# Modulation vectors as TensorE products, a reordered seven-product scheme, and an earlier start of the second FFN half

## The chip, the cores and the metric

One core of one Trainium2 chip. The metric is the device time of one execution, in microseconds (us). TensorE (PE) multiplies matrices, VectorE (DVE) and GpSimd (POOL) work elementwise, ScalarE (ACT) applies functions and copies, SyncE (SP) issues the DMAs, in the order of its one queue.

## The reference, cut to what matters

Two blocks run one after the other on a sequence of 512 tokens of width 1024. The first has two layers of FFN, attention mix, FFN on the sequence and on a context of 256 tokens; the second has a recurrent and a stick-breaking layer and is not touched. What the change touches:

```python
c_act, cc_act = silu(c), silu(c_ctx)                     # two vectors of 1024
mod   = (c_act  @ w_mod[layer] + b_mod[layer])           # 9 vectors of 1024 a layer
mod_c = (cc_act @ w_mod[layer] + b_mod[layer])           # the same for the context
y = swiglu(modulate(rms_norm(h, g_pre), shift, scale), w1, w2)   # silu(gate) * up, then @ w2
h = h + 0.5 * gate * rms_norm(y, g_post)                 # hidden width 2816 = 22 blocks of 128
```

## The kernel before, in words

Everything is fp32. A large product is three fp32r products of a high and a low part (`mm3`, L415): each weight tile is cast by ScalarE into its high part (L348) and the rest is formed by VectorE or GpSimd (L354) in a ring of 8 tiles `op`. Weights come through a ring of 4 tiles `raw`. TensorE runs its instructions in the order in which the program emits them; a small planner with a clock of its own (`run`) interleaves generators for it. The other engines and the SP queue get their order from the framework's scheduler.

Four FFN sublayers take part, called F1 to F4 here: (layer 0, sub 0), (0, 2), (1, 0), (1, 2). Each walks its 22 hidden blocks in groups of 4, 4, 4, 3, 3, 4 (`ffn`, L694). The first group is computed plainly (`ffn1`, `ffn2`), beside the norms that are still pending. For the other five groups, `strassen` (L734) forms every hidden block from seven half-size products of twelve matmuls each, 84 in all: 384 columns wide in F1 to F3, 256 in F4. `wsums` (L386) forms the sums of weights they need. VectorE joins the products (L738, L749) while four PSUM banks b1 to b4 are reused: b1, b3 and b4 take a second product once VectorE or ScalarE has read the first. Then `ffn2` multiplies the group's blocks with the second weight matrix (the "second half" of the group below), eight output tiles m, for the context (256 columns) and the sequence (512); output tile m = 0 is begun with all blocks but the last.

The modulation vectors for later sublayers are made in the background. `tick` (L427), called between blocks and between output tiles, starts a piece of `mods` (L597): two loads of 512 KB of `w_mod` come through the `raw` ring, and VectorE multiplies it by one element of `c` per partition and adds it into `macc` (L624, L626), some instructions at a time (`drip`, L434). TensorE then sums `macc` over the partitions by a product with ones (L634), and four transposes (L647) bring the vector into feature order. The first two vectors of layer 0 are made otherwise (`mods0`, L569): products of 32 columns of `c` with 512 columns of `w_mod`, four side by side in the array (`tile_position`), L578.

Of the kernel before, what the change touches and what calls it, by code (L numbers as in the profile page):

```python
# [11 lines left out]
F32 = mybir.dt.float32  # L12
# [100 lines left out]
def layout(inp):  # L113
# [7 lines left out]
    o["wmodA"] = np.ascontiguousarray(wm[0, ..., : 2 * D])  # L121
    o["wmodB"] = np.ascontiguousarray(wm.reshape(2, 2, 4, P, 18, 512).transpose(0, 4, 1, 3, 2, 5))
# [142 lines left out]
class Builder:  # L265
    def __init__(self, ctx, tc, I, O):
        self.ctx, self.tc, self.nc, self.I, self.O = ctx, tc, tc.nc, I, O
        self.const = self.pool(ctx, "const")
        self.wp = self.pool(ctx, "wp")
        self.tmp = self.pool(ctx, "tmp")  # L270
        self.ps = ctx.enter_context(tc.tile_pool(name="ps", bufs=1, space=PSUM))
        self.wide = None
        self.open_wide()
        self.bg, self.drips = [], []
# [111 lines left out]
    def wsums(self, src):  # L386
# [16 lines left out]
        add(s1, a21, a22)  # L403
        add(s2, s1, a11)
        o2 = put(s2, False)
        add(a21, a11, a21)
        o3 = put(a21, True)
        o4 = put(a12, False)
        add(s2, s2, a12)
        o5 = put(s1, True)  # L410
        o6 = put(a22, True)
        o7 = put(s2, True)
# [21 lines left out]
    def drip(self, n):  # L434
        for f in self.drips[:n]:
            f()
        del self.drips[:n]
# [131 lines left out]
    def mods0(self, pool, hook):  # L569
# [4 lines left out]
        def step(k):  # L574
            raw = pool.tile([P, 2048], F32, name="raw", tag="raw", bufs=7)
            self.dma(raw, I["wmodA"][k])
# [20 lines left out]
    def mods(self, vectors):  # L597


        nc, I = self.nc, self.I  # L600
        box = {}

        def step(l, q, u, half):
            nv = 1 if l == 1 and q > 4 else 2
            if u == half == 0:
                box["po"] = self.po()
            raws = []

            def load():
                raws.append(self.raw())  # L610
                self.dma(raws[-1].rearrange("p (k c) -> p k c", k=2), I["wmodB"][l, 2 * q + u, half][:, 2 * len(raws) - 2 : 2 * len(raws)])

            load()
            if half == 0:
                box["acc"] = self.sums.tile([P, 2, 512], F32, name="macc", tag="macc", bufs=1)
            acc = box["acc"]

            def part(kk, v):
                k = 4 * half + kk
                if kk == 1 and v == 0:  # L620
                    load()
                w, c = raws[kk // 2][:, 512 * (kk % 2) : 512 * (kk % 2) + 512], self.cT[:, k, v : v + 1]
                if k == 0:
                    nc.vector.tensor_scalar(out=acc[:, v, :], in0=w, scalar1=c, scalar2=None, op0=ALU.mult)  # L624
                else:
                    nc.vector.scalar_tensor_tensor(out=acc[:, v, :], in0=w, scalar=c, in1=acc[:, v, :], op0=ALU.mult, op1=ALU.add)  # L626

            return [lambda kk=kk, v=v: part(kk, v) for kk in range(4) for v in range(nv)]

        def reduce(l, q, u):  # L630
            nv = 1 if l == 1 and q > 4 else 2
            po = box["po"][:, 256 * u : 256 * u + 256]
            for j in range(2 * nv):
                nc.tensor.matmul(po[32 * j : 32 * j + 32, :], lhsT=self.ones[:, 0:32], rhs=box["acc"][:, j % nv, j // nv * 256 : j // nv * 256 + 256],  # L634
                                 start=True, stop=True, tile_position=(0, 32 * j))
            if u:
                m = 64 * nv
                box["row"] = self.ftile(512, "row")
                nc.vector.tensor_copy(box["row"][:m, :], box["po"][:m, :])

        def finish(l, q):
            nv = 1 if l == 1 and q > 4 else 2
            m = 64 * nv
            row = box["row"]
            tp = self.pt()
            for b in range(4):
                nc.tensor.transpose(tp[:, b * P : b * P + m], row[:m, b * P : (b + 1) * P], self.ident[:m, :m])  # L647
            src = tp.rearrange("p (u b j w) -> p u b j w", u=2, b=2, w=32)
            two = lambda t: t.rearrange("p (h b) -> p b h", h=2)
            for v in range(nv):  # L650
                for u in range(2):
                    sl = slice(8 * q + 4 * u, 8 * q + 4 * u + 4)
                    nc.vector.tensor_tensor(out=two(self.modc[l][:, v, sl]), in0=src[:, u, :, v : 2 * nv : nv, 0],
                                            in1=two(self.small1[:, 72 * l + 8 * q + 4 * u :][:, :4]), op=ALU.add)
            if q % 3 == 1:
                self.mod_finish(l, q // 3)
            if q % 3 == 2:
                self.mod_gate(l, q // 3)

        def do(red, fin, now):  # L660
            if red:
                reduce(*red)
            if fin is not None:
                finish(*fin)
            return step(*now) if now else []

        out, last = [], None
        for x in vectors:
            for u in range(2):
                out.append(lambda a=last, b=(*x, u, 0): do(a, None, b))  # L670
                out.append(lambda a=last[:2] if last and not u else None, b=(*x, u, 1): do(None, a, b))
                last = (*x, u)
        out.append(lambda: do(last, None, None))
        out.append(lambda: do(None, last[:2], None))
        return out
# [18 lines left out]
    def ffn(self, l, sub, firsts, parts, joint, lasts, pend, exits, spill=None, lag=0):  # L694
# [6 lines left out]
        with self.tc.tile_pool(name=f"ffn{l}{sub}", bufs=1, reuse_waits="tile") as pool:  # L701
            self.fpool = self.sums = pool
            self.open_wide(True)
            i0 = off = 0
# [29 lines left out]
    def strassen(self, pool, l, wi, i0, mids, h):  # L734
# [4 lines left out]
        new = lambda nm: pool.tile([P, n], F32, name=nm, tag=nm, bufs=2)  # L739
        for ii, mid in enumerate(mids):  # L740
            A = self.wsums(self.I["wf1"][l, wi, i0 + ii])
            b1, b2, b3, b4 = (self.bank()[:, :n] for _ in range(4))

            def mm(i, p, b, start):
                yield from self.mm3(p, A[i], [(k, *x) for k, x in enumerate(b)], start=start, more=not start)
                self.drip(1)
# [8 lines left out]
            yield from mm(1, b2, h.T2, True)  # L755
            v = new("v")
            sub(v, b2, c)
            yield from mm(2, b3, h.T3, True)
            u = new("u")
            sub(u, v, b3)  # L760
            yield from mm(3, b1, h.B21, False)
            sg = pool.tile([P, 512], F32, name="sg", tag="sg", bufs=2)[:, :n]
            nc.scalar.activation(sg, b1, AF.Silu)
            yield from mm(4, b4, h.T1, True)
            sub(u, u, b4)
            yield from mm(5, b3, h.T4, False)
            m = self.ftile(n, "m")
            sub(m, v, b3)
            emit(0, m, sg)
            yield from mm(6, b4, h.B22, False)  # L770
# [4 lines left out]
            if ii % 2 == 0:  # L775
                yield from self.tick()

    def ffn1(self, pool, l, wi, i0, mids, ss, ticks=False):
        nc = self.nc
        for ii, mid in enumerate(mids):  # L780
# [3 lines left out]
            for w in (wg, wu):  # L784
                for st in ss:
                    p = self.pg()[:, : st.n]
                    yield from self.mm3(p, w, st.rhs())
                    if w is wg:
                        sg = pool.tile([P, 512], F32, name="sg", tag="sg", bufs=2)[:, : st.n]
# [6 lines left out]
                    if ticks:  # L796
                        self.drip(2)
# [3 lines left out]
    def ffn2(self, l, wi, off, mids, ss, first, last, ticks, cb=None):  # L801
        nc = self.nc
        n = 2 * len(mids) * P
        for m2 in range(4):
# [3 lines left out]
            for mm in range(2):  # L808
                m = 2 * m2 + mm
                rhs = lambda st: [(i, t[:, 0, st.cs], t[:, 1, st.cs]) for i, t in enumerate(mids)]  # L810
                ps = [self.pg()[:, : st.n] for st in ss] if m == 0 else []
                for st, p in zip(ss, ps):
                    yield from self.mm3(p, ws[mm], rhs(st)[:-1], stop=False)
                for i, st in enumerate(ss):
                    if m == 0:
                        p = ps[i]
# [11 lines left out]
                    if ticks:  # L828
                        self.drip(4 // len(ss))
# [408 lines left out]
    def block1(self):  # L1238
# [67 lines left out]
        pend = self.ffn(0, 0, first, [lat], both, both, pend, links(0, 0, 0, 1), lambda out: spill(out, True))  # L1306
        assert not self.bg
        pend = self.mix(0, both, both, pend, [link(cx, 0, 1, 0, 2), halves(0, 1, 0, 2)])
        self.bg += self.mods([(0, 8)] + [(1, q) for q in range(4)])
        pend = self.ffn(0, 2, first, [lat], both, both, pend, [link(cx, 0, 2, 1, 0), halves(0, 2, 1, 0)], spill)  # L1310
        assert not self.bg
        self.bg += self.mods([(1, q) for q in range(4, 8)])
        pend = self.ffn(1, 0, first, [lat], both, both, pend, links(1, 0, 1, 1), spill)
        assert not self.bg
        self.bg += self.mods([(1, 8)])
# [631 lines left out]
```

## Time and profile before

| | |
|---|---|
| time, median of 3 runs (lowest to highest) | 3959.23 us (3951.5 to 3959.98) |
| profiled execution: its time, its span | 3959.93 us, 3958.2 us |
| busy in the span: PE, DVE, ACT, POOL | 89%, 71%, 43%, 38% |
| mean granted clock of TensorE | 0.949 |
| VectorE busy on `macc` (L624, L626) | 382 us in 448 instructions |

The profiled execution has 1.7 us outside its span. The time of a stretch is compared with what its matmuls take when nothing is waited for; the rest is waiting, a lower clock, or small other work.

### The profile page before, as it was taken

What the parts mean: (1) busy time and instruction counts of PE and PEld (TensorE: products, weight loads), DVE (VectorE), ACT (ScalarE), POOL (GpSimd) and SP (SyncE); (2) the same over time, 40 slices, a digit from 0 to 9 for tenths busy, and PEclk for the clock granted to TensorE, in tenths of its full rate; (3) what the DMA queues carried; (4) which work ended last, traced back from release to release, by engine and by line L of the source; (5) the groups of instructions that cost most, each with busy time, mean ns of one, the idle gap of its engine ahead of it and who ended that gap; (6) DMA issues with size and microseconds to landing.
All of it is one profiled execution on the core that took longest, in us unless ns stands there. A gap on an engine that the chain in (4) does not pass through costs nothing. (4 is left out here: it accounts for less than half of the span.)

```text
span 3958.2 us, 61299 instructions
## 1 busy us (share of the span) xinstructions
PE 3529.9 (89%) x23004; PEld 3168.0 (80%) x23004; DVE 2821.9 (71%) x5221; ACT 1693.7 (43%) x3591; POOL 1491.1 (38%) x1191
## 2 busy tenths in 40 slices
PE   7798888999979898988999988988999888899997
PEld 6688788777778887877888976777888787899886
DVE  6977787766787878688767577667756777556446
ACT  5422224556543322344222344554334545535544
POOL 4534344321244433435434432124545434334112
PEclk8999999999989999989999989999999989999998
DMA  7333333312242323433333241133323320234112
GB/s 254 117 101 110 109 112 130 108 61 85 94 134 91 123 92 116 136 128 111 107 107 120 72 146 59 62 101 112 115 88 109 113 80 28 86 103 144 59 49 75
DMA packets 125440, 410.39 MB, mean 104 GB/s; under 512 B 14035, under 2 KB 25814, under 8 KB 123350
## 3 DMA queue, kind: packets, MB, share of 16 engines
q1 hardware_dynamic: 125142, 406.47, 31.8%
q8 instruction: 180, 2.95, 0.3%
q14 instruction: 118, 0.97, 0.1%
HBM read 397.90 MB, written 8.52 MB: 103 GB/s over the span
## 5 line engine op out<-in xcount | busy, mean ns | idle before, releaser
L354 POOL TENSOR_TENSOR op<-raw,op 128x512 fp32r<-128x512 f32 (+1 forms) x660 | 928.0, 1407 | 1595.3 <-ACT op L348 1459.9
L348 ACT CAST op<-raw 128x512 fp32r<-128x512 f32 (+2 forms) x1178 | 702.9, 606 | 796.3 <-DMA raw<-wf 351.8
L354 DVE TENSOR_TENSOR op<-raw,op 128x512 fp32r<-128x512 f32 (+2 forms) x518 | 447.7, 866 | 198.0 <-ACT op L348 194.9
L422 PE MATMUL pg<-h,op 128*128 128x256 f32 (+1 forms) x1440 | 477.4, 332 | 56.8 <-ACT sg L790 20.5
L422 PE MATMUL pg<-mid,op 128*128 128x256 f32 (+1 forms) x1264 | 453.7, 359 | 45.5 <-ACT mid L348 37.6
L424 PE MATMUL pg<-h,op 128*128 128x256 f32 (+1 forms) x1440 | 460.6, 320 | 12.5 <-DVE op L354 10.3
L423 PE MATMUL pg<-h,op 128*128 128x256 f32 (+1 forms) x1440 | 466.5, 324 | 5.7 <-DVE h L534 4.4
L423 PE MATMUL pg<-mid,op 128*128 128x256 f32 (+1 forms) x1264 | 447.1, 354 | 15.4 <-POOL mid L354 10.8
L424 PE MATMUL pg<-mid,op 128*128 128x256 f32 (+1 forms) x1264 | 443.2, 351 | 0.6 <-POOL op L354 0.6
L417 PE MATMUL bank<-h,op 128*128 128x384 f32 (+1 forms) x1704 | 319.2, 338 | 59.3 <-DVE u L738 53.7
L422 PEld LDWEIGHTS pg<-h,op 128*128 128x128 f32 x1440 | 291.3, 202 | 78.4 <-ACT sg L790 21.7
L626 DVE SCALAR_TENSOR_TENSOR macc<-raw,cT,macc 128x512 f32<-128x512 f32 x392 | 344.5, 908 | 12.4 <-DMA raw<-wmodB 11.7
L417 PEld LDWEIGHTS bank<-h,op 128*128 128x128 f32 x1704 | 293.4, 197 | 69.1 <-DVE u L738 31.0
L422 PEld LDWEIGHTS pg<-mid,op 128*128 128x128 f32 x1264 | 247.6, 196 | 99.0 <-ACT mid L348 45.3
L424 PEld LDWEIGHTS pg<-h,op 128*128 128x128 f32 x1440 | 291.2, 202 | 28.0 <-DVE op L354 11.3
L423 PEld LDWEIGHTS pg<-h,op 128*128 128x128 f32 x1440 | 290.9, 202 | 25.3 <-DVE h L534 13.1
L423 PEld LDWEIGHTS pg<-mid,op 128*128 128x128 f32 x1264 | 248.0, 196 | 49.8 <-POOL mid L354 15.6
L424 PEld LDWEIGHTS pg<-mid,op 128*128 128x128 f32 x1264 | 247.9, 196 | 31.8 <-POOL op L354 1.1
L825 DVE TENSOR_TENSOR y<-pg,y 128x256 f32<-128x256 f32 (+1 forms) x288 | 161.0, 560 | 144.1 <-PE pg L424 141.7
L354 POOL TENSOR_TENSOR op<-ws,op 128x512 fp32r<-128x512 f32 x142 | 212.8, 1499 | 129.3 <-ACT op L348 128.4
L348 ACT CAST op<-ws 128x512 fp32r<-128x512 f32 x213 | 131.8, 619 | 279.0 <-DVE ws L394 178.5
L422 PE MATMUL bank<-h,op 128*128 128x384 f32 (+1 forms) x636 | 208.1, 327 | 0.0
(427 smaller groups left out, 8545.5 us busy)
## 6 DMA issues: line engine op xcount, KB each, us to landing
raw<-wf SPq DMA_DIRECT2D x326, 512.0 KB, 3.8
raw<-wmodB SPq DMA_DIRECT2D x128, 512.0 KB, 3.8
raw<-win SPq DMA_DIRECT2D x58, 512.0 KB, 3.7
raw<-ewin SPq DMA_DIRECT2D x48, 512.0 KB, 3.7
raw<-owin SPq DMA_DIRECT2D x40, 512.0 KB, 3.7
raw<-wout SPq DMA_DIRECT2D x32, 512.0 KB, 3.6
raw<-wf SPq DMA_DIRECT2D x32, 384.0 KB, 3.2
raw<-ewout SPq DMA_DIRECT2D x24, 512.0 KB, 3.6
```

Of the source, the lines that this page charges most:

```text
L348: self.nc.scalar.copy(hi, src)
L354: eng.tensor_tensor(out=lo, in0=src, in1=hi.bitcast(F32), op=ALU.subtract)
L417: mm = self.nc.tensor.matmul if not more else lambda *a, **kw: self.nc.tensor.matmul(*a, skip_group_check=True, **kw)
L422: mm(p, lhsT=a, rhs=xh, start=start and i == 0, stop=False)
L423: mm(p, lhsT=a, rhs=xl, start=False, stop=False)
L424: mm(p, lhsT=b, rhs=xh, start=False, stop=stop and i == len(rhs) - 1)
L626: nc.vector.scalar_tensor_tensor(out=acc[:, v, :], in0=w, scalar=c, in1=acc[:, v, :], op0=ALU.mult, op1=ALU.add)
L825: nc.vector.tensor_tensor(out=y, in0=p, in1=y, op=ALU.add)
```

## The change

Three edits, all in the FFN sublayers:

- `mods` makes two vectors at a time as products on TensorE, the way `mods0` does. A step is 1 MB of `w_mod` (128 rows of two vectors) in two tiles `mraw` of their own and four products of 32 x 512 columns into `po`; eight steps make a pair, then ScalarE copies `po` to `row`, and at the next tick four transposes follow. The tiles for step i + 1 are loaded behind the matmuls of step i, into the same two tiles. The first load of an FFN is emitted at its start. `tick` runs one step; `strassen` calls it after every block (before: every second one), `ffn2` as before after its first three tile pairs. `drip` goes. The vector (1, 8), made in F4 before, is made in F3.
- `strassen` runs its seven products in another order: B11, T1, T2, T3, B21, B22, T4 (before B11, T2, T3, B21, T1, T4, B22), with `wsums` in the matching order. The half of the block that needs no second Silu comes last, and the last block of a group gets its low part from VectorE instead of GpSimd.
- `ffn2` begins output tile m = 1, too, with all blocks but the last, in PSUM banks of the `bank` ring.

```diff
 def wsums(self, src):
         add(s1, a21, a22)
+        o2 = put(s1, True)
         add(s2, s1, a11)
-        o2 = put(s2, False)
+        o3 = put(s2, False)
...
 def tick(self):
-        self.drip(99)
         if self.bg:
-            self.drips = self.bg.pop(0)()
-            yield 0.5
+            self.bg.pop(0)()
+            yield 0.9
...
+    def mods(self, pairs):
+        todo = [(pr, k) for pr in pairs for k in range(KD)]
+        def load(i):
+            pr, k = todo[i]
+            box[i] = [self.sums.tile([P, 1024], F32, name="mraw", tag="mraw", bufs=2) for _ in range(2)]
+            for t, (l, q) in zip(box[i], pr):
+                self.dma(t, I["wmod"][l, k][:, D * q : D * (q + 1)])
+        def step(i):
+            k = todo[i][1]
+            if k == 0:
+                box["po"] = self.po()
+            if i not in box:
+                load(i)
+            raws = box.pop(i)
+            for j in range(4):
+                nc.tensor.matmul(box["po"][32 * j : 32 * j + 32, :], lhsT=self.cT[:, k, :], rhs=raws[j // 2][:, 512 * (j % 2) : 512 * (j % 2) + 512],
+                                 start=k == 0, stop=k == KD - 1, tile_position=(0, 32 * j))
+            if k == KD - 1:
+                box["row"] = self.stile(512)
+                nc.scalar.copy(box["row"], box["po"])
+            if i + 1 < len(todo):
+                load(i + 1)
...
 def strassen(self, pool, l, wi, i0, mids, h):
-        new = lambda nm: pool.tile([P, n], F32, name=nm, tag=nm, bufs=2)
+        new = lambda nm: pool.tile([P, n], F32, name=nm, tag=nm, bufs=1)
...
-                self.split(mid[:, 0, c0 : c0 + n], mid[:, 1, c0 : c0 + n], a, True)
+                self.split(mid[:, 0, c0 : c0 + n], mid[:, 1, c0 : c0 + n], a, ii < len(mids) - 1)
...
+            yield from mm(1, b4, h.T1, True)
+            yield from mm(2, b2, h.T2, True)
             v = new("v")
             sub(v, b2, c)
             u = new("u")
-            sub(u, v, b3)
+            sub(u, v, b4)
+            yield from mm(3, b3, h.T3, True)
+            sub(u, u, b3)
+            yield from mm(4, b1, h.B21, False)
...
+            yield from mm(5, b4, h.B22, False)
             m = self.ftile(n, "m")
             sub(m, b4, v)
             nc.scalar.activation(m, m, AF.Silu)
             emit(n, u, m)
-            if ii % 2 == 0:
-                yield from self.tick()
+            yield from mm(6, b3, h.T4, False)
+            m = self.ftile(n, "m")
+            sub(m, v, b3)
+            emit(0, m, sg)
+            yield from self.tick()
...
 def ffn2(self, l, wi, off, mids, ss, first, last, ticks, cb=None):
-                ps = [self.pg()[:, : st.n] for st in ss] if m == 0 else []
-                for st, p in zip(ss, ps):
-                    yield from self.mm3(p, ws[mm], rhs(st)[:-1], stop=False)
+                if m == 0:
+                    ps = {(x, i): (self.bank if x else self.pg)()[:, : st.n] for x in range(2) for i, st in enumerate(ss)}
+                    for (x, i), p in ps.items():
+                        yield from self.mm3(p, ws[x], rhs(ss[i])[:-1], stop=False)
...
 def block1(self):
-        self.bg += self.mods([(0, q) for q in range(2, 8)])
+        self.bg, loads = self.mods([((0, q), (0, q + 1)) for q in (2, 4, 6)])
...
+        self.bg, loads = self.mods([((0, 8), (1, 0)), ((1, 1), (1, 2)), ((1, 3), (1, 4))])
...
+        self.bg, loads = self.mods([((1, 5), (1, 6)), ((1, 7), (1, 8))])
```

## Rows read from the trace of the kernel before

**Rows 1.** The page's busy times: busy us, share of the span, instructions.

```profile
PE 3529.9 (89%) x23004; PEld 3168.0 (80%) x23004; DVE 2821.9 (71%) x5221; ACT 1693.7 (43%) x3591; POOL 1491.1 (38%) x1191
```

**Rows 2.** Windows, the 15 seven-product stretches of F1 to F3: length, busy (instructions).

```profile
290.80:361.90 71.10, 61.73 (x350) 59.34 (x349) 62.24 (x78) 25.82 (x50) 38.21 (x27) 1.00 0.37 117
...
2229.20:2288.40 59.20, 59.20 (x337) 59.16 (x337) 34.35 (x45) 24.81 (x46) 30.93 (x25) 1.00 0.32 102
sum 912.60, PE 846.07 PEld 823.44 DVE 668.63 ACT 341.00 POOL 495.37; mean PE 56.40 PEld 54.90 DVE 44.58 ACT 22.73 POOL 33.02
```

**Rows 3.** The same windows, instructions on tile macc alone: length, PE, PEld, DVE.

```profile
290.80:361.90 71.10, 0.64 (x8) 0.16 (x8) 21.90 (x23) 1.00 0.37 117
...
2229.20:2288.40 59.20, 0.00 (x0) 0.00 (x0) 0.00 (x0) 1.00 0.32 102
sum 912.60, PE 8.00 PEld 1.94 DVE 160.68; mean PE 0.53 PEld 0.13 DVE 10.71
```

**Rows 4.** Windows, the 12 second halves between those stretches; columns as in rows 2.

```profile
sum 425.80, PE 392.31 PEld 321.40 DVE 314.42 ACT 52.09 POOL 74.19; mean PE 32.69 PEld 26.78 DVE 26.20 ACT 4.34 POOL 6.18
```

**Rows 5.** Waits of PE from 183 to 2342 us: us in total, times, longest.

```profile
PE bank L417 <- DVE u L738: 51.2, 23, 5.1
...
PE pg L422 <- ACT mid L348: 22.0, 12, 3.7
...
PE pg L423 <- POOL mid L354: 9.8, 15, 0.7
```

**Rows 6.** Waits of PE from 2757 to 3100 us, in F4.

```profile
PE bank L417 <- DVE u L738: 13.3, 11, 2.4
PE pg L422 <- ACT mid L348: 11.0, 4, 3.8
```

**Rows 7.** Timeline of PE behind a wait, then across a sum of two vectors' macc.

```profile
2811.73 0.63 PE L422 MATMUL pg<-mid,op 128*128 128x512 f32 x1
2812.16 0.63 PE L423 MATMUL pg<-mid,op 128*128 128x512 f32 x1
...
2815.09 0.40 PE L423 MATMUL pg<-mid,op 128*128 128x512 f32 x1
2815.33 0.40 PE L424 MATMUL pg<-mid,op 128*128 128x512 f32 x1
2815.65 0.62 PE L634 MATMUL po<-macc,ones 128*32 128x256 f32 x4
2816.21 0.50 PE L422 MATMUL pg<-mid,op 128*128 128x512 f32 x1
```

**Rows 8.** Timeline of PE: the same sum with four column groups, in F1.

```profile
263.19 0.64 PE L634 MATMUL po<-macc,ones 128*32 128x256 f32 x8
263.76 0.39 PE L422 MATMUL pg<-mid,op 128*128 128x256 f32 x1
```

**Rows 9.** Timeline of PE at the start: steps of mods0 (a step is x8).

```profile
19.37 4.01 PE L578 MATMUL po<-raw,cT 128*32 128x512 f32 x24
...
30.02 1.94 PE L578 MATMUL po<-raw,cT 128*32 128x512 f32 x8 [4.24 <-DMA raw<-wmodA]
```

**Rows 10.** Windows, F4: sums over its 5 seven-product stretches, then its 4 second halves.

```profile
sum 190.10, PE 176.76 PEld 173.75 DVE 130.24 ACT 92.28 POOL 124.78; mean PE 35.35 PEld 34.75 DVE 26.05 ACT 18.46 POOL 24.96
...
sum 101.40, PE 89.41 PEld 68.05 DVE 55.95 ACT 25.45 POOL 36.59; mean PE 22.35 PEld 17.01 DVE 13.99 ACT 6.36 POOL 9.15
```

**Rows 11.** Window, the first group of F1, all instructions; columns as in rows 2.

```profile
81.90:183.80 101.90, 77.47 (x497) 69.14 (x497) 96.30 (x142) 43.82 (x91) 52.80 (x36) 0.93 0.40 132
```

**Rows 12.** DMA issues: count, KB each, median us from issue to landing.

```profile
raw<-wf SPq DMA_DIRECT2D x326, 512.0 KB, 3.8
...
ac<-xc SPq DMA_DIRECT2D x2, 1024.0 KB, 3.9
xc<-ac SPq DMA_DIRECT2D x2, 1024.0 KB, 6.2
```

**Rows 13.** Waits of the SP queue over the span: us in total, times, longest.

```profile
SPq L286 <- DVE op L354: 2452.9, 467, 29.3
```

More of the change, by code (lines that the diff above doesn't have):

```diff
@@ L575, in step @@
             raw = pool.tile([P, 2048], F32, name="raw", tag="raw", bufs=7)
-            self.dma(raw, I["wmodA"][k])
+            self.dma(raw, I["wmod"][0, k][:, : 2 * D])
             for j in range(4):
@@ L595, in mods0 @@
         return out
-    def mods(self, vectors):
+    def mods(self, pairs):
         nc, I = self.nc, self.I
         box = {}
-        def step(l, q, u, half):
-            nv = 1 if l == 1 and q > 4 else 2
-            if u == half == 0:
-                box["po"] = self.po()
[L607 to L644, printed above, removed]
@@ L645, in finish @@
+        def finish(pr):
             tp = self.pt()
             for b in range(4):
[L647 to L672, printed above, removed]
@@ L673, in mods @@
-        out.append(lambda: do(last, None, None))
-        out.append(lambda: do(None, last[:2], None))
-        return out
+                nc.tensor.transpose(tp[:, b * P : (b + 1) * P], box["row"][:, b * P : (b + 1) * P], self.ident)
+            src = tp.rearrange("p (b j w) -> p j b w", b=4, w=32)
+            for i, (l, q) in enumerate(pr):
+                for v in range(1 if l == 1 and q > 4 else 2):
+                    nc.vector.tensor_tensor(out=self.modc[l][:, v, 8 * q : 8 * q + 8].rearrange("p (j b) -> p j b", b=4), in0=src[:, 2 * i : 2 * i + 2, :, v],
+                                            in1=self.small1[:, 72 * l + 8 * q :][:, :8].rearrange("p (j b) -> p j b", b=4), op=ALU.add)
+                if q % 3 == 1:
+                    self.mod_finish(l, q // 3)
+                if q % 3 == 2:
+                    self.mod_gate(l, q // 3)
@@ L677, in mod_finish @@
+        out = []
+        for i, (pr, k) in enumerate(todo):
+            out.append(lambda i=i: step(i))
+            if k == KD - 1:
+                out.append(lambda pr=pr: finish(pr))
+        load_first = lambda: load(0)
+        return out, load_first
     def mod_finish(self, l, sub):
@@ L691, in mod_gate, with ffn @@
                                            scalar=1.0 if sub == 1 else 0.5, in1=gq, op0=ALU.mult, op1=ALU.mult)
-    def ffn(self, l, sub, firsts, parts, joint, lasts, pend, exits, spill=None, lag=0):
+    def ffn(self, l, sub, firsts, parts, joint, lasts, pend, exits, spill=None, lag=0, first=None):
         wi = 0 if sub == 0 else 1
@@ L703, in ffn @@
             self.open_wide(True)
+            if first:
+                first()
             i0 = off = 0
@@ L788, in ffn1 @@
                     if w is wg:
[L789 removed]
+                        sg = pool.tile([P, XW // 2], F32, name="sg", tag="sg", bufs=2)[:, : st.n]
                         nc.scalar.activation(sg, p, AF.Silu)
@@ L1302, in block1 @@
             self.dma(self.X[k], self.I["xin"][:, k, :])
-        self.bg += self.mods([(0, q) for q in range(2, 8)])
+        self.bg, loads = self.mods([((0, q), (0, q + 1)) for q in (2, 4, 6)])
         first = [cx, la, lb]
         pend = [self.chain(self.square_x(st), self.pre(st, 0, 0)) for st in (la, lb)]
-        pend = self.ffn(0, 0, first, [lat], both, both, pend, links(0, 0, 0, 1), lambda out: spill(out, True))
+        pend = self.ffn(0, 0, first, [lat], both, both, pend, links(0, 0, 0, 1), lambda out: spill(out, True), first=loads)
         assert not self.bg
         pend = self.mix(0, both, both, pend, [link(cx, 0, 1, 0, 2), halves(0, 1, 0, 2)])
-        self.bg += self.mods([(0, 8)] + [(1, q) for q in range(4)])
-        pend = self.ffn(0, 2, first, [lat], both, both, pend, [link(cx, 0, 2, 1, 0), halves(0, 2, 1, 0)], spill)
+        self.bg, loads = self.mods([((0, 8), (1, 0)), ((1, 1), (1, 2)), ((1, 3), (1, 4))])
+        pend = self.ffn(0, 2, first, [lat], both, both, pend, [link(cx, 0, 2, 1, 0), halves(0, 2, 1, 0)], spill, first=loads)
         assert not self.bg
-        self.bg += self.mods([(1, q) for q in range(4, 8)])
-        pend = self.ffn(1, 0, first, [lat], both, both, pend, links(1, 0, 1, 1), spill)
+        self.bg, loads = self.mods([((1, 5), (1, 6)), ((1, 7), (1, 8))])
+        pend = self.ffn(1, 0, first, [lat], both, both, pend, links(1, 0, 1, 1), spill, first=loads)
         assert not self.bg
-        self.bg += self.mods([(1, 8)])
         pend = self.mix(1, both, [la, lb], pend, [link(st, 1, 1, 1, 2) for st in (la, lb)])
```

41 lines of the change are left out of this document (10 added, 31 removed).

## The prediction

> **What bounds the kernel now.** I read the page's busy times first: TensorE is busy for 89% of the span, VectorE for 71% [rows 1]. That says only that TensorE comes first on average. The change lies in the four FFN sublayers, so I then asked, stretch by stretch, how much longer a stretch lasts than its matmuls need.
>
> The seven-product stretch from 2229 us is the ruler: 59.20 us for 337 recorded matmuls with TensorE busy all the time, that is 0.176 us for a product of 384 columns [rows 2]. The 15 such stretches of F1 to F3 hold 54 blocks of 84 matmuls, 4536 x 0.176 = 797 us, and last 912.6 us. 116 us are lost there. Where does it go? Work on `macc` fills 160.7 us of VectorE in these stretches; the one from 290.8 us has 23 such instructions, 62 us of VectorE in 71 us, and loses 12 us against the ruler's length, while the ruler has none and loses nothing [rows 2, 3]. The table of waits agrees: the longest item is TensorE waiting for VectorE's subtraction at L738, 51.2 us in 23 waits [rows 5]. A bank's second product may not start before that subtraction has read the first, and in the old order B22 leaves it only one product (T4, 2.1 us).
>
> The second halves lose time at their start: output tile 0 runs through all blocks but the last, then waits for the last block's high part (22.0 us in 12 waits) and low part (9.8 us in 15) [rows 5]; in F4 for 11.0 us in 4 [rows 6]. Such a wait costs more than itself: behind one, 512-column matmuls start 0.43 us apart at 2811.7 us and 0.24 us apart by 2815.1 us [rows 7], the lower and the full level of the clock (1.2 and 2.4 GHz); that is up to half of 3.4 us, 1.7 us, lost once more. With 0.24 us for 512 and half of it for 256 columns, the 12 second halves need 42 blocks x 24 x 0.36 = 363 us, and last 425.8: 63 us are lost [rows 4, 7].
>
> **The change part by part.** *The sums leave VectorE, and the new order gives more slack.* With B11, T1, T2, T3, B21, B22, T4 every second product in a bank stands two products behind the subtraction that frees it: T3 and B21 for b4, B21 and B22 for b3, 4.2 us. Both edits act on the same waits, so I price them together. What is left over in a stretch: nothing in the ruler. I take 2 us a stretch, 30 us in all, for casts and copies that are late for other reasons, so 86 us gained. Bounds: nothing left (116 gained) and 4 us each (56).
>
> *The second half begun without its last block, m = 1 too.* With four blocks that puts another 3 x 3 x 0.36 = 3.2 us of work ahead of the wait, with three 2.2 us; the waits are about 2.7 us each (32 over 12) [rows 5]. The last chain also gets shorter: the half that comes last needs no second Silu, and the low part moves from GpSimd to VectorE. The bank it takes is b1's and b4's, read by then. I leave 1 us to each half: 63 - 12 = 51 gained; bounds 25 (the wait halves) and 63. The three last halves, one stream of 256 columns first, get only 3 x 3 x 0.12 = 1.1 us of cover: 5 us gained together, bounds 0 and 8.
>
> *F4* has products of 256 columns, so one product covers only 1.4 us and waits stay without any `macc`: 13.3 us for L738, 11.0 for the last block [rows 6]. Its stretches need 17 x 84 x 0.12 = 171 us of 190, its four halves 14 x 24 x 0.24 = 81 of 101 [rows 7, 10]. Of these 39 us I take 24 as gained, that is the two waits named; bounds 5 and 36.
>
> *First groups.* In F1's, VectorE is busy for 96 of 102 us and `macc` is in it [rows 11]; the window lies on VectorE. I take 10 us (bounds 0 and 22, what VectorE loses over TensorE's 77 is no more). m = 1 begun early helps there as well: 5 us over four sublayers, bounds 0 and 10.
>
> *What TensorE gets.* 8 vector pairs of 8 steps: 64 steps. The trace has the very operation at the start: three steps in 4.01 us, 1.34 us each, partly at the lower clock, and a single step after a pause of 4.24 us takes 1.94 us [rows 9]. The nearer row is the sum of `macc`, in the middle of dense matmuls: with four column groups of 256 columns it moves the next matmul by 0.57 us, with two groups by 0.56 us [rows 7, 8]. So the groups run side by side, and 512 columns take twice that less the fixed part: 1.1 us a step. 64 x 1.1 = 70 us; bounds 0.95 and 1.34, 61 and 86 us. The old sums with ones, 28 x 0.57 = 16 us, are within the losses above already; the halved sets of transposes count as nothing (no gain claimed). The ACT copy of `po` to `row` once per pair has a whole tick until the transposes read it; 8 of them are hidden.
>
> On switching into column groups a rule speaks against the change. The row: from the last full-width matmul to the sum 0.32 us pass against 0.24 between two full ones, so the entry costs 0.08 us [rows 7]. The Trainium skill (TensorEngine Tiling (Array Packing), section Tiling Modes, Key Properties) says that changing the tiling mode, not just the tile, drains the engine; 64 steps would pay twice 64 drains. It gives no price, and the row's is already within my 0.57 us, so the sum stays by both.
>
> *The loads.* The same 64 MB come, 1 MB a step, into two tiles that are free only when the previous step's matmuls are done. Queued behind such a DMA on SP are the next weights; behind a late one, TensorE's step itself, and all matmuls after it. The next tick is a block away in a seven-product stretch, 14.8 + 1.1 us, but only two output tiles in a second half: 24 x 0.36 = 8.6 us with four blocks, 6.5 with three, and the step's 1.1 us. A DMA of 1 MB lands in 3.9 to 6.2 us, 512 KB in 3.8 [rows 12]. So the load fits unless the queue is late; I count nothing, cover 1 to 6 us in the halves and about 10 in the stretches. In return the weights have the `raw` ring to themselves.
>
> *Sum.* -86 - 51 - 5 - 24 - 10 - 5 + 70 = -111 us. Against the profiled execution's 3959.9 us (0.7 us above the median) that is 3849; I forecast **3850 us** (2.8% faster). With all gains at their low and the steps at their high bound: -56 - 25 - 0 - 5 - 0 - 0 + 86 = 0; with all at the other ends -116 - 63 - 8 - 36 - 22 - 10 + 61 = -194. They won't fall together; about half of each side holds for this case alone, 3795 to 3895.
>
> **The rivals.** *Late loads.* SP waits 5.3 us on average for a weight tile (2452.9 over 467), 29.3 at the longest, and a load behind it waits too [rows 13]. 5.3 + 6 = 11.3 us against 9.7 and 7.6: short by 1.7 and 3.7 us for the steps that follow a tick of a second half, some 28 of 64, 76 us with no lower clock counted. That gives 3925. For it: the longest waits. Against it: those waits are mostly SP running ahead of free tiles, and in the halves few weights are outstanding.
>
> *Slower: the loads block the next block's weights.* If the queue keeps the program's order, a load stands ahead of the weights of the following block, waiting for TensorE's step at the end of the current one. Then those weights start only there: at least the 3.8 us until they land [rows 12] with TensorE idle at each of some 33 ticks inside stretches, and 1.7 us of lower clock behind each: 182 us, 4032, casts not counted. From 3.4 us a tick on (111 over 33) the kernel is slower than before. Against it: the scheduler orders this queue, not the program. For it: nothing in the trace shows that order for a load that waits on TensorE.
>
> *VectorE was not the cause.* If the waits at L738 stay with what VectorE still does, only the second halves gain: 70 - 51 - 5 - 5 and perhaps 30 of the stretches: about 3959, no change. Against it: the ruler.
>
> *More than forecast.* Hardly anything is left over in any stretch: 3785.
>
> **How the numbers follow.** Forecast case 0.60, late loads 0.18, blocked weights 0.09, no cause 0.05, more than forecast 0.08. The range takes in the forecast's own (3795 to 3895) and late loads up to 3930 and leaves the blocked weights and part of the others out: 3790 to 3930. What a measurement of this kernel can tell from no change is about 0.2%, 8 us. Faster by more than that: all of 0.60 and 0.08, nearly all of late loads, a little of no cause, 0.87; within it 0.05; slower 0.08.
>
> **What would show it.** In the profile after: no `macc`, VectorE below 65% busy; stretches of four blocks of 61 to 65 us with four steps in them, each step moving the next matmul by about 1.1 us; waits for L738 in F1 to F3 below 15 us, waits for the last block's `mid` near zero except where 256 columns come first. The prediction is wrong if steps wait for the DMA of `mraw` (late loads), if the first cast of a block waits for the DMA of `wf` with TensorE idle (blocked weights), if a step moves the next matmul by more than 1.4 us, or if L738 still holds TensorE without `macc`.

## The result and the profile after

The changed kernel takes 3797.36 us (median of 4 runs, 3790.61 to 3801.48); the kernel before, timed beside it, 3959.61 us (median of 4). The ratio is 0.959 (95% interval 0.9568 to 0.9612): 162 us gained, where the forecast of 3850 us had 110. The time lies in the range, 7 us above its lower end. Line numbers shift a little: L738 of before is L704, L348 is L347, L354 is L353, L422 is L421; the steps' products are at L611.

The page's busy times, which answer to [rows 1]:

```profile
span 3799.7 us, 61164 instructions
...
PE 3504.7 (92%) x23260; PEld 3128.4 (82%) x23260; DVE 2364.0 (62%) x4769; ACT 1708.1 (45%) x3599; POOL 1400.0 (37%) x1151
```

VectorE lost 458 us of work, TensorE 25, and the span 158. That alone doesn't say where the time came from; the windows do. First the 15 seven-product stretches of F1 to F3, as in [rows 2]:

```profile
271.10:334.90 63.80, 63.80 (x370) 59.45 (x368) 29.91 (x49) 25.22 (x46) 31.79 (x25) 1.00 0.40 128
...
2101.20:2160.90 59.70, 59.33 (x337) 59.01 (x336) 29.57 (x45) 25.16 (x46) 32.08 (x25) 1.00 0.33 102
...
sum 843.10, PE 842.36 PEld 802.12 DVE 398.59 ACT 339.97 POOL 417.52; mean PE 56.16 PEld 53.47 DVE 26.57 ACT 22.66 POOL 27.83
```

The first row has four steps in it and lasts 4.6 us longer than the ruler of [rows 2], 59.20 us: a stretch now lasts as long as its matmuls and its steps, of 1.2 us each (below). In all 15, TensorE is busy for 842.4 of 843.1 us. The 116 us that were lost in [rows 2] are down to 843.1 - 797 - 36 steps x 1.2 = 3. In 66.5 of the 116 TensorE was idle (912.6 - 846.1); part of the rest was the lower clock, since the granted clock was 0.93 to 0.98 in ten of the 15 stretches before, and is 1.00 in all of them now. The 12 second halves between them (answering to [rows 4]), the 3 last halves, and F4's stretches and halves (answering to [rows 10]):

```profile
sum 387.30, PE 386.99 PEld 313.79 DVE 178.24 ACT 69.90 POOL 76.91; mean PE 32.25 PEld 26.15 DVE 14.85 ACT 5.82 POOL 6.41
...
sum 140.10, PE 112.61 PEld 94.99 DVE 124.61 ACT 66.25 POOL 40.93; mean PE 37.54 PEld 31.66 DVE 41.54 ACT 22.08 POOL 13.64
...
sum 184.20, PE 175.54 PEld 173.43 DVE 108.41 ACT 94.98 POOL 130.78; mean PE 35.11 PEld 34.69 DVE 21.68 ACT 19.00 POOL 26.16
...
sum 84.90, PE 80.33 PEld 62.66 DVE 53.21 ACT 22.91 POOL 28.25; mean PE 20.08 PEld 15.66 DVE 13.30 ACT 5.73 POOL 7.06
```

The 12 halves hold 24 steps and last 387.3 us, with TensorE busy for 387.0: next to nothing is lost. The last halves took 154.7 us before:

```profile
sum 154.70, PE 120.02 PEld 100.78 DVE 124.28 ACT 67.42 POOL 47.27; mean PE 40.01 PEld 33.59 DVE 41.43 ACT 22.47 POOL 15.76
```

TensorE's longest waits from 170 to 3060 us (us in total, times, longest):

```profile
PE bank L489 <- DVE dg L484: 34.5, 10, 4.6
...
PE bank L416 <- DVE u L704: 9.4, 12, 2.6
...
PE pg L421 <- ACT mid L347: 4.2, 4, 2.5
```

The head of [rows 5] is gone: what leads now belongs to the mixes and the norms. Of the 9.4 us for L704, 8.7 lie in F4, with its 256 columns. A step on TensorE's timeline (start, length, engine, line):

```profile
285.33 0.68 PE L416 MATMUL bank<-tx,op 128*128 128x384 f32 x3
285.94 1.06 PE L611 MATMUL po<-mraw,cT 128*32 128x512 f32 x8
286.94 0.44 PE L421 MATMUL bank<-h,op 128*128 128x384 f32 x1
287.22 0.34 PE L422 MATMUL bank<-h,op 128*128 128x384 f32 x1
287.40 0.34 PE L423 MATMUL bank<-h,op 128*128 128x384 f32 x1
```

From its start to the next matmul 1.00 us pass. That is not all it costs. The last matmul before it starts at 285.68 us, two of 0.176 us behind 285.33, so the step starts 0.26 us behind it instead of 0.18; and the second matmul behind it comes 0.28 us after the first instead of 0.18. Together that makes 1.2 us. The distance between two steps in a stretch says the same: 15.97 us, for 84 matmuls that take 14.76 by the ruler. No step waits for its load: the 512 KB of `w_mod` land in 4.7 us in the median, and what the engine idles before a step is put down to no releaser ("issue") and to no DMA.

```profile
mraw<-wmod SPq DMA_DIRECT2D x128, 512.0 KB, 4.7
...
its engine sat idle before it (us, times) until:
  issue: 17.7, 60
```

Place by place, from the windows:

| | before | after | measured | forecast |
|---|---|---|---|---|
| stretches F1 to F3 (36 steps) | 912.6 | 843.1 | -69.5 | -86 + 40 = -46 |
| 12 second halves (24 steps) | 425.8 | 387.3 | -38.5 | -51 + 26 = -25 |
| 3 last halves | 154.7 | 140.1 | -14.6 | -5 |
| F4 | 291.5 | 269.1 | -22.4 | -24 |
| first groups (4 steps) | | | -19 | -15 + 4 = -11 |
| the rest (mixes, other layers) | | | +6 | 0 |

### The profile page after: what moved, and what is told of

Its sections match the earlier page's. It is cut to its first block, busy times and chain, and to the rows that moved or that the text cites. A ratio compares the mean times of both kernels' runs of the same rounds, so it can differ in the third digit from the quotient of the medians.

```text
span 3799.7 us, 61164 instructions
## 1 busy us (share of the span) xinstructions
PE 3504.7 (92%) x23260; PEld 3128.4 (82%) x23260; DVE 2364.0 (62%) x4769; ACT 1708.1 (45%) x3599; POOL 1400.0 (37%) x1151
## 4 chain that ended last, share of the span: by engine, by line
PE 53%; DVE 15%; issue 5%; ACT 5%; POOL 2%; DMA 1%; ACTq 0%; DVEq 0%; POOLq 0%; SPq 0%
PE pg L421 9%; PE pg L422 9%; PE pg L423 9%; PE bank L416 7%; PE bank L421 4%; PE bank L423 3%; PE bank L422 3%; DVE op L353 2%; DVE ss L450 1%; PE po L611 1%; POOL op L353 1%; ACT op L347 1%; PE po L844 1%; PE psw L868 1%; PE po L1830 1%
## 5 line engine op out<-in xcount | busy, mean ns | idle before, releaser
L353 POOL TENSOR_TENSOR op<-raw,op 128x512 fp32r<-128x512 f32 (+1 forms) x660 | 891.2, 1351 | 1488.2 <-ACT op L347 1259.1
L347 ACT CAST op<-raw 128x512 fp32r<-128x512 f32 (+2 forms) x1178 | 709.9, 606 | 821.8 <-PE pg L423 421.3
L353 DVE TENSOR_TENSOR op<-raw,op 128x512 fp32r<-128x512 f32 (+2 forms) x518 | 402.6, 779 | 224.2 <-ACT op L347 217.7
L421 PE MATMUL pg<-h,op 128*128 128x256 f32 (+1 forms) x1440 | 480.1, 333 | 61.7 <-DVE m L758 26.5
L422 PE MATMUL pg<-h,op 128*128 128x256 f32 (+1 forms) x1440 | 467.9, 325 | 4.6 <-DVE h L527 3.3
L421 PE MATMUL pg<-mid,op 128*128 128x512 f32 (+1 forms) x1106 | 386.3, 349 | 13.6 <-ACT mid L347 5.3
L422 PE MATMUL pg<-mid,op 128*128 128x512 f32 (+1 forms) x1106 | 379.2, 343 | 1.8 <-DVE mid L353 1.7
L423 PE MATMUL pg<-mid,op 128*128 128x512 f32 (+1 forms) x1106 | 378.8, 342 | 0.0
L421 PEld LDWEIGHTS pg<-h,op 128*128 128x128 f32 x1440 | 293.6, 204 | 86.7 <-DVE m L758 29.2
L422 PEld LDWEIGHTS pg<-h,op 128*128 128x128 f32 x1440 | 292.7, 203 | 23.2 <-DVE h L527 11.1
L416 PE MATMUL bank<-h,op 128*128 128x384 f32 (+1 forms) x1704 | 293.5, 327 | 9.4 <-DVE u L704 9.4
L353 POOL TENSOR_TENSOR op<-ws,op 128x512 fp32r<-128x512 f32 x142 | 191.7, 1350 | 276.8 <-ACT op L347 276.8
L416 PEld LDWEIGHTS bank<-h,op 128*128 128x128 f32 x1704 | 280.9, 190 | 12.3 <-DVE u L704 12.3
L421 PEld LDWEIGHTS pg<-mid,op 128*128 128x128 f32 x1106 | 208.4, 188 | 75.0 <-DVE y L788 29.2
L788 DVE TENSOR_TENSOR y<-pg,y 128x256 f32<-128x256 f32 (+1 forms) x252 | 141.1, 562 | 198.2 <-PE pg L423 197.6
L422 PEld LDWEIGHTS pg<-mid,op 128*128 128x128 f32 x1106 | 208.6, 189 | 27.0 <-DVE mid L353 3.5
L423 PEld LDWEIGHTS pg<-mid,op 128*128 128x128 f32 x1106 | 208.3, 188 | 26.1
L421 PE MATMUL bank<-h,op 128*128 128x384 f32 (+1 forms) x636 | 206.4, 324 | 0.0
L423 PE MATMUL bank<-h,op 128*128 128x384 f32 (+1 forms) x636 | 203.6, 320 | 0.0
L422 PE MATMUL bank<-h,op 128*128 128x384 f32 (+1 forms) x636 | 203.6, 320 | 0.0
```

The costliest lines, as they stand in the source:

```text
L347: self.nc.scalar.copy(hi, src)
L353: eng.tensor_tensor(out=lo, in0=src, in1=hi.bitcast(F32), op=ALU.subtract)
L416: mm = self.nc.tensor.matmul if not more else lambda *a, **kw: self.nc.tensor.matmul(*a, skip_group_check=True, **kw)
L421: mm(p, lhsT=a, rhs=xh, start=start and i == 0, stop=False)
L422: mm(p, lhsT=a, rhs=xl, start=False, stop=False)
L423: mm(p, lhsT=b, rhs=xh, start=False, stop=stop and i == len(rhs) - 1)
```

## The experiments

The question was not whether the kernel got faster but which edit did it, since the prediction priced two of them together, and whether the loads would have mattered. Theory: the sums on VectorE held TensorE up, in stretches and halves. Rivals: the order or the early half did the work and the sums were incidental; or the products cost little only because the loads are hidden. The three edits were run one at a time on the kernel before, and two of them were undone on the kernel after. The runs on the kernel after, from `after_old_order` to `one_tile`, were timed in another session, beside which the kernel before took 3949.91 us, 10 us less than beside the result; where their medians are compared with the 3797.36 us of after, the ratios put them some 8 to 9 us further from it.

**The products alone** (`mods_only`): after, with the old order and the old `ffn2`.

```diff
-            yield from mm(1, b4, h.T1, True)
-            yield from mm(2, b2, h.T2, True)
+            yield from mm(1, b2, h.T2, True)
...
+            yield from mm(2, b3, h.T3, True)
...
-                if m == 0:
-                    ps = {(x, i): (self.bank if x else self.pg)()[:, : st.n] for x in range(2) for i, st in enumerate(ss)}
+                ps = [self.pg()[:, : st.n] for st in ss] if m == 0 else []
```

> The kernel before with the modulation vectors as products on TensorE alone (old order of the seven products, second half begun with one output tile only). Theory: the sums on VectorE made the subtractions of L738 late, and with them gone the 15 seven-product stretches of F1 to F3 fall from 913 us to 843 us as in the kernel after (4 steps of 1.0 us in a stretch of four blocks included); the starts of the second halves and F4 stay as before. About -70 -12 (first group of F1) -10 = 3865 us. Rival: the order and the early second half carry the gain and the products only cost TensorE time: 3930 us or more, with waits at L738 above 40 us.

Measured: 3858.79 us, ratio 0.9752 (0.9736 to 0.9768), -99 us. The windows, stretches and then second halves:

```profile
sum 841.80, PE 841.80 PEld 802.43 DVE 465.35 ACT 330.43 POOL 410.74; mean PE 56.12 PEld 53.50 DVE 31.02 ACT 22.03 POOL 27.38
...
sum 406.40, PE 393.66 PEld 313.17 DVE 173.49 ACT 76.57 POOL 101.45; mean PE 32.81 PEld 26.10 DVE 14.46 ACT 6.38 POOL 8.45
```

In the stretches this edit alone does all that the three do (841.8 against 843.1). In the halves it does half of it, its 24 steps included.

**The order alone** (`order_only`): before, with the new `strassen` order and `wsums`, `drip` and its ticks kept. As in the change, `u` and `v` have one buffer each instead of two (no subtraction or product on VectorE waits for one to come free), and the last block's low part goes to VectorE, so the run prices these together with the order.

```diff
-        new = lambda nm: pool.tile([P, n], F32, name=nm, tag=nm, bufs=2)
+        new = lambda nm: pool.tile([P, n], F32, name=nm, tag=nm, bufs=1)
...
-            b1, b2, b3, b4 = (self.bank()[:, :n] for _ in range(4))
+            b1, b4, b2, b3 = (self.bank()[:, :n] for _ in range(4))
...
-                self.split(mid[:, 0, c0 : c0 + n], mid[:, 1, c0 : c0 + n], a, True)
+                self.split(mid[:, 0, c0 : c0 + n], mid[:, 1, c0 : c0 + n], a, ii < len(mids) - 1)
...
+            yield from mm(5, b4, h.B22, False)
...
+            yield from mm(6, b3, h.T4, False)
```

> The kernel before with the new order of the seven products alone. Theory: with the sums still on VectorE, which then has more work than fits in a block, two products of slack instead of one catch only part of the waits: -15 in F1 to F3, -8 in F4, and some from the shorter last chain, about 3930 us. Rival: the slack was the matter, the waits at L738 vanish with the sums still there: 3880 us or less.

Measured: 3941.97 us, ratio 0.997 (0.9955 to 0.9985), -16 us. The stretches and the last halves, then the wait that the order should have shortened, from 184 to 2331 us:

```profile
sum 914.30, PE 840.79 PEld 819.34 DVE 668.08 ACT 339.75 POOL 483.66; mean PE 56.05 PEld 54.62 DVE 44.54 ACT 22.65 POOL 32.24
...
sum 143.60, PE 115.34 PEld 95.78 DVE 128.40 ACT 67.27 POOL 40.99; mean PE 38.45 PEld 31.93 DVE 42.80 ACT 22.42 POOL 13.66
...
PE bank L417 <- DVE u L738: 62.9, 26, 6.3
```

The stretches stay at 914.3 us and the wait grows, from the 51.2 us of [rows 5]. Two products of slack do not help while VectorE has 668 us of work in 914. That the sums make the subtraction late, and not its place in the block, is argued here and shown by `sums_left_out` below. What the order gives lies in the last halves (-11), F4 (-10) and the second halves (-3.4).

**The early half alone** (`half_only`): before, with the new `ffn2`.

```diff
+                if m == 0:
+                    ps = {(x, i): (self.bank if x else self.pg)()[:, : st.n] for x in range(2) for i, st in enumerate(ss)}
```

> The kernel before with the second half begun with two output tiles without their last block, alone. Theory: the waits for the last block's high and low part (32 us in F1 to F3, 12 in F4) and the lower clock behind them go, nothing else: about -45, 3915 us. Rival: what is won at the start of a half is lost in the next stretch, since VectorE is behind with the sums anyway: 3945 us or more.

Measured: 3905.67 us, ratio 0.9876 (0.9856 to 0.9896), -52 us. The second halves:

```profile
sum 406.40, PE 386.45 PEld 319.63 DVE 310.91 ACT 51.98 POOL 75.85; mean PE 32.20 PEld 26.64 DVE 25.91 ACT 4.33 POOL 6.32
```

They shorten by 19 us without any help from the other edits; 8 us of the last halves, 12 of F4's and 10 of the stretches come with it. The single edits give 99, 16 and 52 us, 167 together, against 162: in total they add up within the noise (the intervals are 6 to 9 us to either side), though not place by place, as the next ones show.

**The sums left out** (`sums_left_out`): before, with 392 of the 448 instructions on `macc` removed, loads and products with ones kept. The vectors are not the reference's.

```diff
-                else:
-                    nc.vector.scalar_tensor_tensor(out=acc[:, v, :], in0=w, scalar=c, in1=acc[:, v, :], op0=ALU.mult, op1=ALU.add)
```

> The kernel before with 392 of the 448 VectorE instructions of the modulation sums left out (only the first product of each sum is formed, so the vectors are not the reference's); loads, reductions and all else stay. Theory: this alone takes the waits of the seven-product stretches away, and since the other VectorE instructions also get shorter when VectorE and GpSimd have less to do at a time, the stretches of F1 to F3 fall from 913 us to below 820; about -110, 3850 us. Rival: VectorE's own work of the seven products is the cause: 3920 us or more.

Measured: 3847.0 us, ratio 0.9724 (0.9707 to 0.9741). The stretches:

```profile
sum 809.70, PE 809.70 PEld 801.40 DVE 460.45 ACT 325.78 POOL 402.85; mean PE 53.98 PEld 53.43 DVE 30.70 ACT 21.72 POOL 26.86
```

103 us go with one deleted statement, and TensorE is busy to the last digit. Loads, banks and order are those of before, so the sums on VectorE were the cause in the stretches. Against this run the stretches of `mods_only` cost 842 - 810 = 32 us more, for 36 steps less the old sums with ones, which are still in here.

One path to the same cause stays open. `w_mod` took up to two of the four `raw` tiles until its sums were formed. In the stretches of before VectorE, on top of its work on `macc`, idled for 31.1 us until weights and for 8.2 us until `w_mod` had landed; here it idles for 2.8 us, and in `mods_only`, where `w_mod` has tiles of its own, for 1.3. So the sums may have made L738 late partly through late weights, which no run separates from the time in the queue. In after, late weights do not hold TensorE up: VectorE idles 28.0 us for them in the stretches, and next to nothing is lost.

**After with the old order** (`after_old_order`; the edit of `order_only` undone, but for the single buffers).

> The kernel after with the old order of the seven products. Theory: without the sums VectorE is on time even with one product of slack, so F1 to F3 lose next to nothing in the stretches; F4 (products of 1.4 us) loses some 6 us, and the longer last chain some 10 us at the starts of the second halves: about +15, 3812 us. Rival: the order is a main cause: 3835 us or more.

Measured: 3807.31 us, ratio 0.9636 (0.9621 to 0.9651): 10 us over after by the medians, 18 by the ratios. Stretches 842.5 us, last halves 145.8. Second halves:

```profile
sum 387.50, PE 386.93 PEld 313.85 DVE 173.45 ACT 76.52 POOL 101.51; mean PE 32.24 PEld 26.15 DVE 14.45 ACT 6.38 POOL 8.46
```

**After with the old half** (`after_old_half`; the edit of `half_only` undone).

> The kernel after with the second half begun with output tile 0 only. Theory: 2 to 4 us at each of the 12 starts in F1 to F3, the same at four in F4, the lower clock included: about +40, 3837 us. Rival: the new order's shorter chain had already taken these waits away: +10 or less.

Measured: 3817.44 us, ratio 0.9664 (0.9639 to 0.969). Second halves:

```profile
sum 389.10, PE 388.62 PEld 313.47 DVE 179.70 ACT 69.54 POOL 77.23; mean PE 32.38 PEld 26.12 DVE 14.98 ACT 5.79 POOL 6.44
```

That is 20 us over after by the medians and 29 by the ratios, against the 40 expected: the early half is worth less here than on the kernel before. With the sums gone, either edit alone makes the halves whole: 387.5 with the early half, 389.1 with the new order, 387.3 with both, and 406.4 with neither (`mods_only`). The shorter last chain and the longer cover remove the same wait. What the early half still gives on top of the order lies in F1's first group (7 us), the last halves and F4.

**Each step's products twice** (`steps_twice`): same loads; the vectors come out doubled.

```diff
+            for x in range(2):
+                for j in range(4):
+                    nc.tensor.matmul(box["po"][32 * j : 32 * j + 32, :], lhsT=self.cT[:, k, :], rhs=raws[j // 2][:, 512 * (j % 2) : 512 * (j % 2) + 512],
+                                     start=k == 0 and x == 0, stop=k == KD - 1 and x == 1, tile_position=(0, 32 * j))
```

> The kernel after with every step's four products issued twice (the vectors without their bias come out doubled). Theory: TensorE is busy without a gap in the stretches and halves where the steps stand, so each doubled step costs what it moves the next matmul by, somewhat less than the 1.0 us of a single one since the entry is paid once: 60 of 64 steps x 0.86 to 1.0 = +52 to +60, about 3853 us. Rival: steps stand in time that is lost anyway: +20 or less.

Measured: 3849.44 us, ratio 0.9743 (0.9728 to 0.9758), 52 us over after, or 0.8 us for each of 64 steps. Of the 52, the windows find 29.5 in the stretches (872.6 us) and 20.5 in the second halves (407.8). A doubled step on the timeline:

```profile
293.61 1.93 PE L612 MATMUL po<-mraw,cT 128*32 128x512 f32 x16
295.46 0.44 PE L421 MATMUL bank<-h,op 128*128 128x384 f32 x1
295.74 0.33 PE L422 MATMUL bank<-h,op 128*128 128x384 f32 x1
```

1.85 us against 1.00: four more products cost 0.85 us. A whole step costs 1.2, so what is left for entering and leaving the column groups is some 0.35 us a step. TensorE's time in steps goes one to one into the kernel's. The Trainium skill (TensorEngine Tiling (Array Packing), section Tiling Modes, Key Properties) says that switching the tiling mode drains the engine. The trace agrees, at some 0.35 us a step or 22 us in 64.

**One tile and no early load** (`one_tile`): each step's two loads go into one tile, and start only when the products before them are done.

```diff
+                if j % 2 == 0:
+                    raw = self.sums.tile([P, 1024], F32, name="mraw", tag="mraw", bufs=1)
+                    l, q = todo[i][0][j // 2]
+                    self.dma(raw, I["wmod"][l, k][:, D * q : D * (q + 1)])
...
-            if i + 1 < len(todo):
-                load(i + 1)
```

> The kernel after with one tile mraw instead of two, so that a step loads its second half only behind the products of its first. Theory: the early load into two tiles is what hides the transfers; here TensorE waits in each of the 64 steps for a DMA that lands in about 4.7 us, with up to 1.7 us of lower clock behind it, 5 to 6.5 us a step: +320 to +420, 4120 to 4220 us, slower than before. Rival: the transfers have so much slack that the queue's order hides them anyway: below 3850 us.

Measured: 4237.31 us, ratio 1.0721 (1.0701 to 1.074), 440 us over after: 6.9 us a step, above all that was expected. TensorE's wait for the load, and a step on the timeline:

```profile
PE po L612 <- DMA mraw<-wmod: 262.6, 64, 9.1
...
317.56 1.05 PE L612 MATMUL po<-mraw,cT 128*32 128x512 f32 x4
322.04 1.92 PE L612 MATMUL po<-mraw,cT 128*32 128x512 f32 x4 [3.42 <-DMA mraw<-wmod]
...
324.49 0.41 PE L423 MATMUL pg<-mid,op 128*128 128x256 f32 x1
324.70 0.41 PE L421 MATMUL pg<-mid,op 128*128 128x256 f32 x1
```

The wait is 4.1 us a step. Behind it 256-column matmuls start 0.21 us apart instead of 0.12, the lower level of the clock; the mean granted clock falls from 0.959 to 0.925. Over the whole span TensorE idles 254 us more than in after, and is busy for 189 us longer (3693.6 against 3504.7) with the same number of matmuls: that is the 443 us between the two spans. The second part holds the lower clock and the second switch into the column groups; no run separates them. The slower rival itself, in which a load holds up the next block's weights, was not tried. But its price for a load that TensorE waits for, 3.8 + 1.7 us, was too low rather than too high: here it is 6.9. After has no such wait, with two tiles loaded a tick ahead.

**Steps in all first groups** (`first_groups`): after, with steps also behind every block of the first groups of F1 to F3, where TensorE waits anyway. This moves 20 of the 64 steps there.

```diff
-                        self.run(pend[i : i + 1], [g1(firsts[i : i + 1], t=l == sub == 0)])
+                        self.run(pend[i : i + 1], [g1(firsts[i : i + 1], t=True)])
...
-            if ticks and ii % 2 == 0:
+            if ticks:
```

> The kernel after with steps also in the first groups of F2 and F3 and behind every block there (eight a sublayer, F1 from four to eight), so that 20 of the 60 steps leave the stretches and halves in which TensorE never waits for groups in which it does. Theory: in the stretches each step costs its 1.0 us, in the first groups part of it falls into waits for VectorE: 10 to 20 us faster than the kernel after, about 3783 us. Rival: the steps stand in TensorE's order in front of matmuls that are late anyway, and push the work VectorE waits for: no change against the kernel after.

> The kernel after once more on the same chip as the version with steps in the first groups, as its measure: 3797 us, 0.959 of before.

Measured: 3785.12 us (5 runs, 3778.94 to 3790.37), ratio 0.9569 (0.9554 to 0.9584), beside after at 3798.84 (4 runs, 3785.27 to 3800.46), ratio 0.9591 (0.9572 to 0.9611). The stretches:

```profile
sum 829.70, PE 828.56 PEld 801.72 DVE 410.87 ACT 337.19 POOL 417.91; mean PE 55.24 PEld 53.45 DVE 27.39 ACT 22.48 POOL 27.86
```

The stretches and second halves (378.0 us) get shorter by 23 us for the 20 steps that left them, and 14 us arrive in the medians: the first groups hide part of the steps, not all. Its median is below that of both kernels; the two intervals still overlap a little, so against the changed kernel it is likely and not settled.

## Why the prediction was right, and where its sizes were off

**Right: what bounds the stretches.** The ruler's reading, that `macc` in VectorE's queue makes L738 late, held: `sums_left_out` alone clears the stretches. The rival that VectorE was not the cause is ruled out, and late loads and blocked weights did not come: no wait of a step for `mraw`, and 3 us lost in 15 stretches. Waits for L738 in F1 to F3 are under 1 us (forecast: below 15).

**The term that was off most: what is left over.** The prediction left 2 us in each stretch and 1 us in each second half, 30 and 12 in all. Measured: some 3 us over the 15 stretches. The 12 halves last 387.3 - 24 x 1.2 = 358 us without their steps, less than the 363 that their matmuls alone were to need: 512 columns were taken at 0.24 us, and start 0.23 us apart in these halves. So the gain there, 67 us without the steps, lies above its bound of 63. The two terms are 27 and 17 us of the 53 between forecast and time, against which the steps took some 6 more than forecast, and the case "hardly anything is left over" is nearer to what happened. The ruler had already shown a stretch that loses nothing; the allowance had no row of its own.

**Mis-sized: the last halves.** Forecast 5, bounds 0 and 8, measured 14.6: outside the bounds. The price counted only the added cover of 1.1 us a half. The shorter last chain, named in the same paragraph, was given no price there, though it gives most: 11 us in `order_only`, low part on VectorE included, and the early half has 8 alone.

**Mis-sized: the first groups.** 19 gained, steps included, against 11 forecast; 13 of it in F1, which lasts 135.2 us from 35.4 on, where before it took 148.3. The gain is net of 4 steps and within the bounds.

**About right, with some luck: the step and F4.** A step costs 1.2 us against 1.1 (bounds 0.95 and 1.34), worth 6 us over 64. Two errors met in it. From the step's start to the next matmul 1.00 us pass, 0.1 less than taken. But the prediction said that the entry of 0.08 us was within its 0.57, which is counted from the sum's start: the entry lies ahead of that, and the slower exit, 0.1 us, behind it. F4 gained 22.4 us against 24, though of the two waits named only one went: 8.7 of 13.3 us stay at L738 and 1.7 of 11.0 for the last block. Its stretches gave 5.9 us of the 13.3 and its halves 16.5 instead of 11.0, so the sum is right by chance. Two slips did not reach the forecast: the trace of before has 32 sums with ones, not 28, and the terms of the rival that VectorE was not the cause add up to 3939 us, not 3959.

**Priced together, and wrongly so.** Sums and order were priced as one because both act on L738. The pair gained 69.5 + 36 x 1.2 = 113 us without the steps, against 86 (bounds 56 and 116), but the reason given for the order fell: alone it does nothing for the stretches of F1 to F3, and with the sums gone it does nothing there either (842.5 without it, 843.1 with it). Beside 3 us in F4's stretches it works through the chain at a group's end, where it overlaps with the early half.

## What to carry to other kernels

When an engine's own waits point to a short instruction on another engine, ask what that engine's queue holds ahead of it: taking most of 160 us of background work out of the queue gave the 103 us that rearranging the consumer did not. A stretch of the same kernel that lacks the suspect work, and loses nothing, was here the better forecast for the others, with no allowance added. Two edits that shorten one wait, one from each side, were here each worth the whole of it alone and little on top of the other; price such edits as a pair at their common place. And a short job on another tiling is priced by how far it moves the matmuls behind it, not from its own start: here 1.2 us instead of 1.0.

## What the runs showed of the hardware beyond the forecast

VectorE's busy time fell by 458 us, though only 382 us of instructions on `macc` left it. Instructions of the same form and number became shorter. The weight sums of one form, before and then after, in the table of groups (count | busy us, mean ns | idle before):

```profile
L394 DVE TENSOR_TENSOR ws<-ws,raw 128x512 f32<-128x512 f32 x142 | 153.2, 1079 | 10.6 <-POOL op L354 8.5
```

```profile
L393 DVE TENSOR_TENSOR ws<-ws,raw 128x512 f32<-128x512 f32 x142 | 112.5, 792 | 108.5 <-POOL op L353 106.4
```

The shortest (674 and 676 ns), the median (693 and 692) and the longest (1782 and 1768) are alike in both: fewer of them fell into the long kind. In `mods_only`, with the order of before, the mean is 795 ns, in `sums_left_out` 909, and in `order_only`, which has all of VectorE's work, 944, so it depends on what runs beside them and not on the amount of work alone. The traces say what that is. Before, 61 of the 142 take over 1 us, and each of the 61 has a GpSimd instruction beside it for more than half of its time; of the other 81, 59 have none at all. After, 16 take over 1 us, again each with GpSimd beside it for more than half of its time, and 77 of the other 126 have none. The Trainium skill (SBUF — State Buffer, section SBUF: two separate sides) says that a VectorE instruction with two SBUF inputs and a GpSimd instruction take a shared port pair by an exclusive lock, and that the one that comes second is blocked while the first holds it for its whole instruction. The long kind fits that, but no run here varied GpSimd's work by itself.
